# Input projection of a hybrid encoder block: the first and the last 512 tokens taken slice by slice of features

## The chip, the cores and the metric

The kernel runs on one core of one Trainium2 chip, in one launch. The metric is the device time of a whole execution in microseconds. Before the change it is 2899.7 us, the median of three runs (2899.47, 2899.7 and 2901.88).

## What is computed

One encoder block on x, 2048 tokens of 1024 features, all in float32. Only the first lines bear on the change:

```python
xn = rms_norm(h, ln_mix_g[l])
proj = xn @ w_in[l]                      # 2048 x 2512
y_a = mlstm_group(proj[..., OFF_Q:OFF_K], ..., proj[..., OFF_G:OFF_CQ] + b_gates[l], ...)
y_b = mla_group(proj[..., OFF_CQ:OFF_CKV], proj[..., OFF_CKV:OFF_KR], proj[..., OFF_KR:IN_COLS], ...)
```

The last 464 columns of `proj`, called "rest" here, are 16 gate columns, 256 columns of c_q, 128 of c_kv and 64 for the rotary key. `mla_group` applies an RMS norm to c_q and c_kv, and a rotary embedding to the 64. Then come attention, the mLSTM, the output projection, a gated MLP with convolution and a per-layer embedding; the change leaves these alone.

## The kernel before

Tokens stand in 16 tiles of 128 and features in 8 slices of 128. A float32 product is made of three matmuls in a faster 32-bit format: each operand is split into a high part (a cast on ScalarE) and a low part (the difference, on VectorE), and `mm3` (L131) issues low x high, high x low, high x high. The gain of the norm is multiplied into the weights while they are split (`split_g`, L125), and the factor of a token, r = (mean of x^2 + eps)^-1/2, is multiplied in when a product leaves PSUM. A column of these factors is called `rcol`.

`in_proj` (L176) multiplies the same x with three groups of weights one after the other: rest (464 columns), V and O (512 each). Products go to four PSUM banks, `bk`, used in turn. For the rest group the loop of L303 has a step for each token tile:

- `load_x` (L221) loads the turned tile of x, features on partitions (512 KB, `x_t`), one step ahead, and `split_x` (L242) splits it in two halves of 512 elements (L120 on ScalarE, L123 on VectorE).
- `ssq_x` (L228) makes rcol of the tile before: squares on ScalarE (L231), two additions on VectorE (L233, L234), four small matmuls with a column of ones on TensorE (`ssp`, L237), a scale on VectorE (L239), and a power of -1/2 on GpSimd (L240).
- `rest` (L248) issues the 24 matmuls of the tile two steps back (`nat`, L212) and takes the bank out: two gate writes `gt` on VectorE (L252), the scaled copy `rs` on ScalarE (L255), the load of the rotary table `sc` (L257), two squares with sums `ssq` on ScalarE (L261, L262), three small operations on GpSimd for their reciprocal roots (L263, L141, L143), two normed products `nn` on VectorE (L265, L266), a store of `vv_d`, and seven small rotary operations on VectorE (L269 to L275). The bank is free once `gt` and `rs` have read it.
- `turn_rest` (L278), four steps back, transposes the four blocks of `nn` on TensorE into `rtp` (L281), copies them out on ScalarE as `rt` (L283), and stores `rest_d` (256 KB).

After the loop rcol is stored to `r_d` (L320, 2048 single elements), and the V and O groups run 16 tiles of 24 matmuls each; two of the turns stand in the V group. The code's order is a priority: the framework's scheduler places each instruction on its engine's queue, and each queue is then executed in order. All loads and stores are issued on SyncE's queue (SP). `gates()` is a generator of side work on the gate columns that is advanced between the V and O tiles.

Of the kernel before, what the change touches and what calls it, by code (L numbers as in the profile page):

```python
# [19 lines left out]
P = 128  # L20
S = 2048
D = 1024
KT = D // P
NT = S // P
# [3 lines left out]
OFF_V = 1024  # L28
OFF_O = 1536
OFF_R = 2048  # L30
NREST = W_IN_COLS - OFF_R
# [2 lines left out]
PLE = 256  # L34
EPS = 1e-6
SB = 512
LAG_T, LAG_X, LAG_R = 1, 2, 2
SIDE = 668
KSCALE = 128.0 ** -0.5
ASCALE = 192.0 ** -0.5  # L40
# [20 lines left out]
class Block:  # L61
# [114 lines left out]
    def in_proj(self):  # L176
        nc, d = self.nc, self.d
# [5 lines left out]
        def load_w(c0, n, before=None):  # L183

            out, raws = [], []

            def load(k2, parts=1):
                raw = self.at(next(rrot), [P, 2, 512], name="wraw")
                for i in range(parts):
                    bs = slice(2 * i // parts, 2 * (i + 1) // parts)  # L190
                    nc.sync.dma_start(raw[:, bs, :n], w_in[k2, :, bs, c0:c0 + n])
                raws.append(raw)
                return raw

            if before:
                load(0, 2)
                before(0)
                load(1, 2)
                before(1)
                load(2)  # L200
                load(3)
            for k2 in range(KT // 2):
                if k2 == len(raws):
                    load(k2)
                raw = raws[k2]
                for b in range(2):
                    w = self.at(next(wrot), [P, 2, 512], F32R, "wsp")
                    self.split_g(raw[:, b, :n], gcol[:, 2 * k2 + b:2 * k2 + b + 1], w[:, 0, :n], w[:, 1, :n])
                    out.append(w)
            return out  # L210
# [10 lines left out]
        def load_x(st):  # L221

            t = self.at(next(rrot) if st else "u2", [P, KT, P], name="x_t")
            if st:
                nc.sync.dma_start(t, d["x_turned"][:, :, st * P:(st + 1) * P])
            return t

        def ssq_x(st, x_t):  # L228

            sq = self.at("w13", [P, KT, P], name="x_sq")  # L230
            nc.scalar.activation(sq, x_t, AF.Square)  # L231
            ss = self.at("t7", [P, 4, P], name="x_ss")
            nc.vector.tensor_tensor(ss, sq[:, 0:4], sq[:, 4:8], op=ALU.add)  # L233
            nc.vector.tensor_tensor(ss[:, 0:2], ss[:, 0:2], ss[:, 2:4], op=ALU.add)  # L234
            ps = self.pml.tile([P, 4], F32, name="ssp", tag="ml")
            for i in range(2):
                nc.tensor.matmul(ps, ss[:, i], ones, start=i == 0, stop=i == 1)  # L237
            t = self.stat(1, "rsm")
            nc.vector.tensor_scalar(t, ps[:, 0:1], 1.0 / D, EPS, op0=ALU.mult, op1=ALU.add)  # L239
            nc.gpsimd.tensor_tensor(rcol[:, st:st + 1], t, self.nhalf[:, :1], op=ALU.pow)  # L240

        def split_x(st, x_t):  # L242
            c, o = st // 4, (st % 4) * P
            for f in range(2):
                self.split(x_t[:, 4 * f:4 * f + 4], xh[c][f][:, :, o:o + P], xl[c][f][:, :, o:o + P])


        def rest(st):  # L248
            ps = nat(st, ws, NREST)
            rx = rcol[:, st:st + 1]  # L250
            for i, o in ((0, st), (8, NT - 1 - st)):
                nc.vector.scalar_tensor_tensor(self.gt[:, i:i + 8, o], ps[:, i:i + 8], rx, bg[:, i:i + 8],  # L252
                                               op0=ALU.mult, op1=ALU.add)
            rs = self.at(f"t{st % 2}", [P, 448], name="rs")
            nc.scalar.activation(rs, ps[:, 16:NREST], AF.Copy, scale=rx)  # L255
# [5 lines left out]
            nc.scalar.activation(nn[:, 0:256], rs[:, 0:256], AF.Square, scale=1.0 / 16.0, accum_out=ssq[:, 0:1])  # L261
            nc.scalar.activation(nn[:, 256:384], rs[:, 256:384], AF.Square, accum_out=ssq[:, 1:2])  # L262
            nc.gpsimd.tensor_scalar(ssq[:, 1:2], ssq[:, 1:2], 1.0 / 128, None, op0=ALU.mult)  # L263
            r = self.rsq(ssq, 2, 1.0)
            nc.vector.scalar_tensor_tensor(nn[:, 0:256], rs[:, 0:256], r[:, 0:1], gn[:, 0:256], op0=ALU.mult, op1=ALU.mult)  # L265
            nc.vector.scalar_tensor_tensor(nn[:, 256:384], rs[:, 256:384], r[:, 1:2], gn[:, 256:384], op0=ALU.mult, op1=ALU.mult)  # L266
            nc.sync.dma_start(self.vv_d[:, st], nn[:, 256:384])
# [7 lines left out]
            nc.vector.tensor_copy(nn[:, 448:512], nn[:, 384:448])  # L275
            return nn

        def turn_rest(st, nn):  # L278
# [8 lines left out]
        nc.sync.dma_start(gcol, d["g_turned"])  # L287
        rcol = self.cst.tile([P, NT], F32, name="rcol")
        ones = self.cst.tile([P, 4], F32, name="ones")
        nc.vector.memset(ones, 1.0)  # L290
        nq, xq = {}, {}

        xq[0] = load_x(0)

        def first(f):

            fs = slice(4 * f, 4 * f + 4)
            if f < 2:
                nc.sync.dma_start(xq[0][:, fs], d["x_turned"][:, fs, 0:P])
                self.split(xq[0][:, fs], xh[0][f][:, :, 0:P], xl[0][f][:, :, 0:P])  # L300

        ws = load_w(OFF_R, NREST, first)
        for st in range(NT + LAG_X):  # L303
            if st + 1 < NT:
                xq[st + 1] = load_x(st + 1)
            if st == 0:
                gn = self.at("t5", [P, 384], name="gn")
                self.row_bcast(gn[:, 0:256], d["q_norm_g"][0], 256)
                self.row_bcast(gn[:, 256:384], d["kv_norm_g"][0], 128)
                bg = self.row_bcast(self.cst.tile([P, 16], F32, name="bg"), d["b_gates"][0], 16)  # L310
            if 1 <= st < NT:
                split_x(st, xq[st])
            if 0 <= st - 1 < NT:
                ssq_x(st - 1, xq.pop(st - 1))
            if 0 <= st - LAG_X < NT:
                nq[st - LAG_X] = rest(st - LAG_X)
            if 0 <= st - LAG_X - LAG_R < NT:
                turn_rest(st - LAG_X - LAG_R, nq.pop(st - LAG_X - LAG_R))

        nc.sync.dma_start(self.r_d.rearrange("(t p) -> p t", p=P), rcol)  # L320
        gates = self.gates()

        ws = load_w(OFF_V, 512)
        for st in range(NT):
            ps = nat(st, ws, 512)
            if st < LAG_R:
                turn_rest(NT - LAG_R + st, nq.pop(NT - LAG_R + st))
# [3 lines left out]
            if st >= LAG_R:  # L331
                next(gates, None)

        ws = load_w(OFF_O, 512)
# [1709 lines left out]
```

## Time and profile before

| | us |
|---|---|
| median of three runs | 2899.7 |
| the profiled execution's own time | 2898.51 |
| its span in the trace | 2896.7 |
| first matmul of the rest group starts | 7.40 |
| first matmul of the V group starts | 106.63 |
| TensorE busy in the span | 2854.7 |
| VectorE, ScalarE, GpSimd busy | 2029.8, 1524.2, 157.1 |

The granted TensorE clock is 0.998 of full speed. A row of the trace's timeline gives start, duration, engine, line, operation and `out<-in`, and a bracket with the idle time before it and what ended that. The time in which TensorE is busy is summed over matmuls that overlap, so the pace of a stage is read from start to start.

### The profile page before, as it was taken

What the parts mean: (1) busy time and instruction counts of PE and PEld (TensorE: products, weight loads), DVE (VectorE), ACT (ScalarE), POOL (GpSimd) and SP (SyncE); (2) the same over time, 40 slices, a digit from 0 to 9 for tenths busy, and PEclk for the clock granted to TensorE, in tenths of its full rate; (3) what the DMA queues carried; (4) which work ended last, traced back from release to release, by engine and by line L of the source; (5) the groups of instructions that cost most, each with busy time, mean ns of one, the idle gap of its engine ahead of it and who ended that gap; (6) DMA issues with size and microseconds to landing.
All of it is one profiled execution on the core that took longest, in us unless ns stands there. A gap on an engine that the chain in (4) does not pass through costs nothing.

```text
span 2896.7 us, 41145 instructions
## 1 busy us (share of the span) xinstructions
PE 2854.7 (99%) x14622; PEld 2416.9 (83%) x14622; DVE 2029.8 (70%) x3758; ACT 1524.2 (53%) x3014; POOL 157.1 (5%) x295
## 2 busy tenths in 40 slices
PE   8999999999999999999999999999999999999998
PEld 7888888888888889888788888888888788888787
DVE  7521555777777777776777877867777867676787
ACT  7311544556666666665755555655556333254665
POOL 3100000000000010001000000000000000011111
PEclk9999999999999999999999999999999999999999
DMA  6512545653332333378844554657766757576764
GB/s 189 132 59 77 162 125 163 218 162 117 105 111 98 97 104 113 126 244 267 276 145 165 193 174 147 220 176 235 234 230 210 241 187 249 166 265 205 263 217 163
DMA packets 408318, 509.00 MB, mean 176 GB/s; under 512 B 34080, under 2 KB 271664, under 8 KB 408112
## 3 DMA queue, kind: packets, MB, share of 16 engines
q1 hardware_dynamic: 408112, 506.37, 53.8%
q8 instruction: 115, 1.88, 0.3%
q14 instruction: 91, 0.75, 0.1%
HBM read 324.16 MB, written 182.12 MB: 175 GB/s over the span
## 4 chain that ended last, share of the span: by engine, by line
PE 58%; DMA 3%; DVE 3%; issue 2%; ACT 2%; POOL 0%; POOLq 0%; SPq 0%; ACTq 0%; DVEq 0%
PE fy L1434 21%; PE fz L1434 14%; PE fx L1434 14%; PE ppv L133 2%; PE fs L133 1%; PE tb L977 1%; DMA opr<-t_d 1%; DMA h_d<-xt 1%; PE bk L914 1%; PE bk L916 1%; PE bk L915 1%; PE bk L917 1%; PE bk L918 1%; DMA opr<-tw_d 1%; DVE op L123 1%
## 5 line engine op out<-in xcount | busy, mean ns | idle before, releaser
L1434 PE MATMUL fz<-op,fw 128*128 128x512 f32 x1968 | 478.8, 391 | 4.5 <-ACT fw L120 4.0
L1434 PE MATMUL fx<-op,fw 128*128 128x512 f32 x1968 | 476.4, 390 | 0.0
L1434 PE MATMUL fy<-op,fw 128*128 128x512 f32 x1968 | 475.3, 390 | 0.6 <-ACT fy L1546 0.6
L1434 PEld LDWEIGHTS fz<-op,fw 128*128 128x128 f32 x1968 | 368.4, 188 | 82.4 <-ACT fw L120 5.4
L1434 PEld LDWEIGHTS fy<-op,fw 128*128 128x128 f32 x1968 | 368.6, 188 | 77.3 <-ACT fy L1546 1.0
L1434 PEld LDWEIGHTS fx<-op,fw 128*128 128x128 f32 x1968 | 368.2, 188 | 76.1 <-ACT fy L1546 0.2
L1434 PE MATMUL fy<-op,fwd 128*128 128x512 f32 (+1 forms) x984 | 238.2, 390 | 1.9 <-DVE uv L1419 1.5
L120 ACT CAST pt<-tb 128x512 fp32r<-128x512 f32 x256 | 147.3, 587 | 172.1 <-PE tb L977 171.5
L133 PE MATMUL bk<-wsp,xh 128*128 128x512 f32 (+1 forms) x768 | 234.3, 386 | 0.0
L919 DVE TENSOR_REDUCE mx<-bk 128x1 f32<-128x512 f32 x256 | 174.8, 684 | 59.8 <-PE bk L918 58.8
L1434 PEld LDWEIGHTS fy<-op,fwd 128*128 128x128 f32 x984 | 182.6, 188 | 40.6 <-DVE uv L1419 2.6
L133 PE MATMUL ppv<-pt,kv 128*128 128x256 f32 x1536 | 205.2, 287 | 0.4 <-DVE pt L123 0.3
L123 DVE TENSOR_TENSOR pt<-tb,pt 128x512 fp32r<-128x512 f32 x256 | 173.9, 683 | 31.4 <-ACT pt L120 29.2
L937 ACT ACTIVATE pe<-bk,nm 128x512 f32<-128x512 f32 x256 | 174.8, 695 | 37.8 <-DVE nm L931 33.0
L133 PEld LDWEIGHTS ppv<-pt,kv 128*128 128x128 f32 x1536 | 189.3, 191 | 0.9 <-DVE pt L123 0.5
L133 PEld LDWEIGHTS bk<-wsp,xh 128*128 128x128 f32 x768 | 145.3, 189 | 25.0
L133 PE MATMUL bk<-wsp,xl 128*128 128x512 f32 (+1 forms) x384 | 150.6, 392 | 7.4 <-DVE xl L123 7.4
L133 PE MATMUL bk<-xh,wqk 128*128 128x512 f32 x480 | 157.1, 393 | 0.0
L977 PE MATMUL tb<-ident,pe 128*128 128x128 f32 x1024 | 151.0, 273 | 3.8 <-DVE pt L123 3.7
L977 PEld LDWEIGHTS tb<-ident,pe 128*128 128x128 f32 x1024 | 121.7, 140 | 23.4 <-DVE pt L123 6.0
L120 ACT CAST fw<-hraw 128x1024 fp32r<-128x1024 f32 (+1 forms) x72 | 70.2, 980 | 115.7 <-PE fx L1434 58.7
L120 ACT CAST op<-opr 128x512 fp32r<-128x512 f32 x165 | 95.9, 621 | 58.3 <-DMA opr<-tw_d 17.6
(360 smaller groups left out, 4915.3 us busy)
## 6 DMA issues: line engine op xcount, KB each, us to landing
fwr<-in_w_up SPq DMA_DIRECT2D x66, 512.0 KB, 5.2
fh<-h_d SPq DMA_DIRECT2D x48, 512.0 KB, 4.3
h_d<-fh SPq DMA_DIRECT2D x48, 512.0 KB, 4.1
s_d<-fwr SPq DMA_DIRECT2D x44, 512.0 KB, 3.2
fws<-s_d SPq DMA_DIRECT2D x44, 512.0 KB, 3.5
rw<-row_d SPq DMA_DIRECT2D x32, 512.0 KB, 5.1
tw_d<-tsum SPq DMA_DIRECT2D x60, 256.0 KB, 5.3
opr<-tw_d SPq DMA_DIRECT2D x60, 256.0 KB, 5.1
```

What stands on the lines that cost most here:

```text
L120: nc.scalar.copy(hi, src)
L123: (sub or nc.vector).tensor_tensor(lo, src, _f(hi), op=ALU.subtract)
L133: mm = lambda *a, **k: self.nc.tensor.matmul(*a, **k, skip_group_check=more)
L914: mm(ps, ql, kh[:, ks], start=True, stop=False)
L915: mm(ps, qr, self.krl[:, ks], start=False, stop=False)
L916: mm(ps, qh, kl[:, ks], start=False, stop=False)
L917: mm(ps, qr, self.kr2[:, ks], start=False, stop=False)
L918: mm(ps, qh, kh[:, ks], start=False, stop=True)
L919: nc.vector.tensor_reduce(s.mx[:, kb:kb + 1], ps, axis=AX.X, op=ALU.max)
L937: nc.scalar.activation(s.pe[:, kb % 2], s.banks[kb], AF.Exp, bias=s.nm, scale=ASCALE, accum_out=s.rs[:, kb:kb + 1])
L977: nc.tensor.transpose(t[:, j, :], s.p[kb][:, j * P:(j + 1) * P], self.ident)
L1434: nc.tensor.matmul(out, a[:, k * P:(k + 1) * P], parts[lo][:, cols], start=first, stop=lo == 1 and k == last, skip_group_check=more)
```

## The change

The rest group is ordered by hand: inside `manual_schedule` TensorE, VectorE and ScalarE keep the order of the code, while SP and GpSimd are still placed by the scheduler. The parts:

- The first four token tiles and the last four are each computed as one block (`block4`): all four banks at once, slice by slice of features, 96 matmuls. For the first block x arrives as 8 slices of 512 tokens (`x_c`, 256 KB each) between the weights' loads, and each slice is split as it is needed. In the last block the V weights are split step by step.
- The other tiles of x arrive by pairs: 256 tokens in two halves of the features (`x_p`, 512 KB each), each split with one cast and one difference of 1024 elements, at written places: the pair of tiles 4 and 5 ahead of the first eviction, the others behind the evictions of tiles 2, 4, 6, 7 and 8.
- rcol is made from a second copy of x, rows of tokens (`x_n`, 512 KB a tile, two buffers): one square on ScalarE of 1024 elements with a sum along the row, then a scale and a power on GpSimd. The additions on VectorE and the `ssp` matmuls are gone.
- The eviction of tile s stands behind the products of tile s+2, with the squares of its rows directly ahead of it. In it the rotary operations stand ahead of the two `nn`.
- The turn of tile s stands ahead of the products of tile s+5; turns 9, 10 and 11 stand inside the last block; the evictions and turns of tiles 12 to 15 stand in the V group, as does the store of `r_d`.
- Eight matmuls of the identity and a one-element activation stand at the start; `gcol` (the gain) is loaded by ScalarE's queue instead of SP's. The side work `gates` is first advanced four V tiles later.

```diff
-        def ssq_x(st, x_t):
-            sq = self.at("w13", [P, KT, P], name="x_sq")
-            nc.scalar.activation(sq, x_t, AF.Square)
-            ss = self.at("t7", [P, 4, P], name="x_ss")
-            nc.vector.tensor_tensor(ss, sq[:, 0:4], sq[:, 4:8], op=ALU.add)
-            nc.vector.tensor_tensor(ss[:, 0:2], ss[:, 0:2], ss[:, 2:4], op=ALU.add)
-            ps = self.pml.tile([P, 4], F32, name="ssp", tag="ml")
-            for i in range(2):
-                nc.tensor.matmul(ps, ss[:, i], ones, start=i == 0, stop=i == 1)
-            t = self.stat(1, "rsm")
-            nc.vector.tensor_scalar(t, ps[:, 0:1], 1.0 / D, EPS, op0=ALU.mult, op1=ALU.add)
-            nc.gpsimd.tensor_tensor(rcol[:, st:st + 1], t, self.nhalf[:, :1], op=ALU.pow)
+        def load_pair(p):
+            for f in range(2):
+                raw = self.at(next(rrot), [P, 4, 256], name="x_p")
+                nc.sync.dma_start(raw, d["x_turned"][:, 4 * f:4 * f + 4, p * 256:(p + 1) * 256])
+                xq[p, f] = raw
+        def load_rows(st):
+            t = xn[st] = self.at(("w13", "u2")[st % 2], [P, D], name="x_n")
+            nc.sync.dma_start(t, d["x"][0, st * P:(st + 1) * P, :])
+        def ssq_x(st):
+            ss = self.stat(1, "x_ss")
+            nc.scalar.activation(self.at("t7", [P, D], BF16, "x_sq"), xn.pop(st), AF.Square, accum_out=ss)
+            self.rsq(ss, 1, 1.0 / D, rcol[:, st:st + 1])
+        def block4(c, step):
+            ps = [self.bank() for _ in range(4)]
+            for kt in range(KT):
+                f, k = divmod(kt, 4)
+                step(kt)
+                w, x = ws[kt], ((xh, 0), (xl, 0), (xh, 1))
+                order = [(n, st) for st in range(4) for n in range(3)]
+                for n, st in order if c or kt else sorted(order):
+                    o, e = x[n]
+                    nc.tensor.matmul(ps[st][:, :NREST], o[c][f][:, k, st * P:(st + 1) * P], w[:, e, :NREST],
+                                     start=kt == 0 and n == 0, stop=kt == KT - 1 and n == 2)
+            done.update(enumerate(ps, 4 * c))
...
+        with self.tc.manual_schedule(engines={ET.PE, ET.DVE, ET.Activation}):
+            for _ in range(8):
+                nc.tensor.matmul(wp, self.ident, self.ident, start=True, stop=True)
+            raws, xr = first_loads()
+            block4(0, first_step)
...
+            ssq_x(0)
+            load_rows(2)
+            load_pair(3)
+            for f in range(2):
+                split_pair(2, f)
+            ssq_x(1)
+            load_rows(3)
+            evict(0)
+            evict(1)
+            loads, splits = {4: 4, 6: 5, 8: 6, 9: 7}, {4: 3, 6: 4, 8: 5, 9: 6, 10: 7}
+            for st in range(4, NT - 4):
+                if st in loads:
+                    load_pair(loads[st])
+                if st > 4:
+                    turn(st - 5)
+                done[st] = nat(st, ws, NREST)
+                ssq_x(st - 2)
+                load_rows(st)
+                evict(st - 2)
+                if st in splits:
+                    for f in range(2):
+                        split_pair(splits[st], f)
+            raws, wv = load_w(OFF_V, 512), []
+            for st in range(NT - 4, NT - 2):
+                turn(st - 5)
+                ssq_x(st - 2)
+                load_rows(st)
+                evict(st - 2)
+            for st in range(NT - 2, NT):
+                ssq_x(st - 2)
+                load_rows(st)
+            block4(3, last_step)
...
+            if st < 4:
+                evict(NT - 4 + st)
+            ps = nat(st, wv, 512)
+            if 2 <= st < 6:
+                turn(NT - 6 + st)
+            if st == 3:
+                nc.sync.dma_start(self.r_d.rearrange("(t p) -> p t", p=P), rcol)
```

More of the change, by code (lines that the diff above doesn't have):

```diff
@@ L181, in in_proj, with load_w, split_w @@
         w_in = d["w_in"][0].rearrange("(a b p) c -> a p b c", b=2, p=P)
[L183 to L201, printed above, removed]
-            for k2 in range(KT // 2):
[L203 to L210, printed above, removed]
+        def load_w(c0, n):
+            raws = []
+            for k2 in range(KT // 2):
+                raws.append(self.at(next(rrot), [P, 2, 512], name="wraw"))
+                nc.sync.dma_start(raws[k2][:, :, :n], w_in[k2, :, :, c0:c0 + n])
+            return raws
+        def split_w(raws, kt, n):
+            w = self.at(next(wrot), [P, 2, 512], F32R, "wsp")
+            self.split_g(raws[kt // 2][:, kt % 2, :n], gcol[:, kt:kt + 1], w[:, 0, :n], w[:, 1, :n])
+            return w
         def nat(st, ws, n):
@@ L242, in split_x @@
-        def split_x(st, x_t):
-            c, o = st // 4, (st % 4) * P
-            for f in range(2):
-                self.split(x_t[:, 4 * f:4 * f + 4], xh[c][f][:, :, o:o + P], xl[c][f][:, :, o:o + P])
-        def rest(st):
-            ps = nat(st, ws, NREST)
+        def load_pair(p):
+            for f in range(2):
+                raw = self.at(next(rrot), [P, 4, 256], name="x_p")
+                nc.sync.dma_start(raw, d["x_turned"][:, 4 * f:4 * f + 4, p * 256:(p + 1) * 256])
+                xq[p, f] = raw
@@ new lines, in split_pair @@
+        def split_pair(p, f):
+            c, o = p // 2, p % 2 * 256
+            self.split(xq.pop((p, f)), xh[c][f][:, :, o:o + 256], xl[c][f][:, :, o:o + 256])
+        def load_rows(st):
[5 more added lines that the diff above has]
+            self.rsq(ss, 1, 1.0 / D, rcol[:, st:st + 1])
@@ new lines, in first_loads @@
+        def first_loads():
+            raws, xr = [], []
+            for kt in range(KT):
+                if kt % 2 == 0:
+                    raws.append(self.at(next(rrot), [P, 2, 512], name="wraw"))
+                xr.append(self.at(f"t{kt}", [P, 512], name="x_c"))
+                if kt < 2:
+                    nc.sync.dma_start(raws[0][:, kt, :NREST], w_in[0, :, kt, OFF_R:OFF_R + NREST])
+                    if kt == 0:
+                        nc.scalar.dma_start(gcol, d["g_turned"])
+                elif kt % 2 == 0:
+                    nc.sync.dma_start(raws[kt // 2][:, :, :NREST], w_in[kt // 2, :, :, OFF_R:OFF_R + NREST])
+                nc.sync.dma_start(xr[kt], d["x_turned"][:, kt, 0:512])
+            load_rows(0)
+            load_pair(2)
+            load_rows(1)
+            return raws, xr
@@ new lines, in block4 @@
+        def block4(c, step):
+            ps = [self.bank() for _ in range(4)]
+            for kt in range(KT):
+                f, k = divmod(kt, 4)
[7 more added lines that the diff above has]
+            done.update(enumerate(ps, 4 * c))
@@ L250, in rest @@
+        def rest(st, ps):
             rx = rcol[:, st:st + 1]
@@ L275, in rest @@
             nc.vector.tensor_copy(nn[:, 448:512], nn[:, 384:448])
+            nc.vector.scalar_tensor_tensor(nn[:, 0:256], rs[:, 0:256], r[:, 0:1], gn[:, 0:256], op0=ALU.mult, op1=ALU.mult)
+            nc.vector.scalar_tensor_tensor(nn[:, 256:384], rs[:, 256:384], r[:, 1:2], gn[:, 256:384], op0=ALU.mult, op1=ALU.mult)
+            nc.sync.dma_start(self.vv_d[:, st], nn[:, 256:384])
             return nn
@@ L286, in in_proj @@
         gcol = self.cst.tile([P, KT], F32, name="gcol")
-        nc.sync.dma_start(gcol, d["g_turned"])
         rcol = self.cst.tile([P, NT], F32, name="rcol")
[L289 to L318, printed above, removed]
@@ L320, in in_proj, with evict, turn, first_step @@
-        nc.sync.dma_start(self.r_d.rearrange("(t p) -> p t", p=P), rcol)
+        warm = self.stat(1, "warm")
+        nc.scalar.activation(warm, self.nhalf[:, 0:1], AF.Copy, scale=2.0)
+        wp = self.pml.tile([P, P], F32, name="warm", tag="ml")
+        nq, xq, xn, done, ws = {}, {}, {}, {}, []
+        ET = mybir.EngineType
+        def evict(st):
+            nq[st] = rest(st, done.pop(st))
+        def turn(st):
+            turn_rest(st, nq.pop(st))
+        def first_step(kt):
+            f, k = divmod(kt, 4)
+            ws.append(split_w(raws, kt, NREST))
+            self.split(xr[kt], xh[0][f][:, k, :], xl[0][f][:, k, :])
@@ new lines, in last_step @@
+        def last_step(kt):
+            if kt in (0, 2):
+                ssq_x(NT - 2 + kt // 2)
+            wv.append(split_w(raws, kt, 512))
+            if kt in (2, 4, 6):
+                turn(NT - 8 + kt // 2)
+        with self.tc.manual_schedule(engines={ET.PE, ET.DVE, ET.Activation}):
[3 more added lines that the diff above has]
+            block4(0, first_step)
+            gn = self.at("t5", [P, 384], name="gn")
+            self.row_bcast(gn[:, 0:256], d["q_norm_g"][0], 256)
+            self.row_bcast(gn[:, 256:384], d["kv_norm_g"][0], 128)
+            bg = self.row_bcast(self.cst.tile([P, 16], F32, name="bg"), d["b_gates"][0], 16)
+            ssq_x(0)
[30 more added lines that the diff above has]
+            block4(3, last_step)
@@ L330, in in_proj @@
             nc.sync.dma_start(self.v_d[st], t)
-            if st >= LAG_R:
+            if st >= 6:
                 next(gates, None)
-        ws = load_w(OFF_O, 512)
+        raws = load_w(OFF_O, 512)
+        ws = [split_w(raws, kt, 512) for kt in range(KT)]
         go = self.row_bcast(self.at("t6", [P, 512], name="go"), d["mlstm_norm_g"][0], 512)
```

13 lines of the change are left out of this document (removed).

## The prediction

> **What bounds the kernel now.** I read the page first, then the busy times of the stretch that the change touches, then TensorE's waits in it.
>
> ```profile
> span 2896.7 us, 41145 instructions
> ...
> PE 2854.7 (99%) x14622; PEld 2416.9 (83%) x14622; DVE 2029.8 (70%) x3758; ACT 1524.2 (53%) x3014; POOL 157.1 (5%) x295
> ```
> ```profile
> 7.40:106.60 99.20, 96.92 (x503) 86.03 (x504) 70.36 (x256) 67.71 (x149) 35.71 (x61) 1.00 0.68 167
> ```
> ```profile
> PE bk L133 <- DVE xl L123: 7.4, 1, 7.4
> PE ssp L237 <- DVE x_ss L234: 2.2, 3, 1.1
> ```
>
> The second row is the rest group: 99.20 us, then busy time (and count) of PE, PEld, DVE, ACT, POOL, then clock, DMA share and GB/s. TensorE (PE) is the bound, 99% in the whole and 96.92 of 99.20 here; it waits 7.4 us for its first operand and 2.2 us later. VectorE (DVE) and ScalarE (ACT) are busy 70%. Everything behind the group is unchanged and PE-bound, so I carry the shift of the V group's start to the end 1:1. How PE spends a steady tile:
>
> ```profile
> 53.60 0.60 PE L281 MATMUL rtp<-ident,nn 128*128 128x128 f32 x4
> 54.04 0.51 PE L237 MATMUL ssp<-ones,x_ss 128*128 128x4 f32 x4
> 54.40 0.45 PE L133 MATMUL bk<-wsp,xl 128*128 128x464 f32 x1
> 59.50 0.60 PE L281 MATMUL rtp<-ident,nn 128*128 128x128 f32 x4
> 106.63 0.48 PE L133 MATMUL bk<-wsp,xl 128*128 128x512 f32 x1
> ```
>
> From start to start a turn takes 0.44, the sums of squares 0.36, the 24 products 5.10 (0.21 each): 5.90 us a tile. The group has 16 x 5.10 + 14 x 0.44 + 16 x 0.36 = 93.5 of its 99.2 us; 5.7 are a slow start and short waits. The V group starts at 106.63.
>
> **What the change takes off PE.** The `ssp` matmuls go: 5.8 us. Two more turns move into V: 0.9 off here, 0.9 on there. The start:
>
> ```profile
> 4.03 1.28 ACT L128 ACT_TABLE_LOAD   x1 [4.03 <-DMA wraw<-in_w_in]
> 5.33 0.68 ACT L128 ACTIVATE wsp<-wraw,gcol 128x464 fp32r<-128x464 f32 x1
> 8.72 0.59 PE L133 MATMUL bk<-wsp,xl 128*128 128x464 f32 x1
> 9.88 0.59 PE L133 MATMUL bk<-wsp,xl 128*128 128x464 f32 x1
> 12.15 0.37 PE L133 MATMUL bk<-wsp,xl 128*128 128x464 f32 x1
> ```
>
> The one-element activation pulls the table load under the first transfer, which lands at 4.03. Then one weight split (0.68) and one cast (0.62, from the row below) give the first product at 4.0 + 0.7 + 0.6 = 5.3 instead of 7.40, as the new order begins with high x high. Three products take 1.16 us until about 12 (8.72 to 9.88), against 0.63 later: over the 4.6 us of the slow start some 2.0 us are lost. The eight identity matmuls are to save these. By the four of 53.60 they last about 1 us warm, 2 cold, and would end two to three us ahead of the first product, while the trace's own products needed 4.6 us of unbroken work. I charge 1.0, half of it, with ends 0 and 2.0.
>
> The Trainium skill ("TensorE: Matmul & The Clock Gate", "Part 1: The HAM clock gate") says full rate follows about 3.4 us of sustained activity in a free-running window; by that rule the identity matmuls do nothing, and the sum would be 1.0 higher.
>
> If PE alone set the time, V would start at 5.3 + 1.0 + 16 x 5.10 + 12 x 0.44 = 93.2, 13.4 us early. The question is whether tiles are evicted fast enough.
>
> **What the written order makes of the eviction.** ScalarE now runs, in this order for each tile: `rt` of an older tile, squares of x rows, `rs`, two squares; behind five of the tiles two casts of 1024. The squares of rows feed GpSimd (POOL), whose power feeds `gt` and `rs` of the same tile. So one tile's eviction begins only after the earlier one's squares, and this ring has these durations:
>
> ```profile
> 24.15 0.35 DVE L252 SCALAR_TENSOR_TENSOR gt<-bk,rcol,bg 128x8 f32<-128x8 f32 x2
> ...
> 24.62 0.63 ACT L255 ACTIVATE rs<-bk,rcol 128x448 f32<-128x448 f32 x1 [1.31 <-DVE gt L252]
> ```
> ```profile
> 54.61 1.28 DVE L123 TENSOR_TENSOR xl<-x_t,xh 128x512 fp32r<-128x512 f32 x2
> ...
> 56.31 0.92 POOL L240 TENSOR_TENSOR rcol<-rsm,nhalf 128x1 f32<-128x1 f32 x1 [2.40 <-DVE rsm L239]
> ...
> 58.07 0.58 ACT L283 COPY rt<-rtp 128x512 f32<-128x512 f32 x1
> ...
> 58.54 0.43 ACT L261 ACTIVATE nn<-rs 128x256 f32<-128x256 f32 x1
> ...
> 59.15 0.20 ACT L262 ACTIVATION_READ_ACCUMULATOR nn<-rs 128x1 f32 x1
> 59.24 1.05 ACT L231 ACTIVATE x_sq<-x_t 128x1024 f32<-128x1024 f32 x1
> ...
> 59.44 0.22 POOL L263 TENSOR_SCALAR ssq<-ssq 128x1 f32<-128x1 f32 x1 [2.21 <-ACT nn L262]
> ...
> 60.02 0.73 POOL L143 TENSOR_TENSOR rsr<-rsm,nhalf 128x2 f32<-128x2 f32 x1
> ...
> 60.19 0.61 ACT L120 CAST xh<-x_t 128x512 fp32r<-128x512 f32 x1
> ```
>
> `gt` to `rs` 0.47; `rs` 0.63; both squares 0.70 (58.54 to 59.24); `rt` 0.47 (58.07 to 58.54); row squares 1.05 and 0.1 for the sum; POOL's scale 0.3 (59.44 to 60.02 holds two such operations); power 0.92; then the next `gt`. Sum 4.64, say **4.6 us**. PE's own step is 5.10 + 0.44 = 5.54, so a tile without a split keeps up. With a split two casts stand ahead of `rt`: a 1024-element pass takes 0.95 from start to start (59.24 to 60.19), so 1.9 more: **6.5 us**. VectorE's two differences, 2.5 us by four halves of 54.61, lie beside that. The old code's split was as much work, but nothing made the tile's `rcol` wait for it. DVE loses the two additions and L239, which were no bound.
>
> From the first `rs` to that of tile 11 are 11 steps, 6 plain and 5 with a split: 27.6 + 32.5 = 60.1 us. The last block needs all four banks, and its fourth is tile 11's, so this ring, not PE, sets when the block can run.
>
> Two terms come on top. First, POOL beside VectorE:
>
> ```profile
> L263 POOL TENSOR_SCALAR ssq<-ssq x16: 222/224/1296, 21.4 to 111.8; 128x1 f32<-128x1 f32 x16
> ```
> ```profile
> 44.47 1.30 POOL L263 TENSOR_SCALAR ssq<-ssq 128x1 f32<-128x1 f32 x1 [0.53 <-ACT nn L262]
> ...
> 45.00 0.68 DVE L123 TENSOR_TENSOR xl<-x_t,xh 128x512 fp32r<-128x512 f32 x1
> ```
>
> The same tiny operation takes 0.22 us at the median and 1.30 at worst (first row: minimum, median, maximum in ns), and the worst ends with the difference that runs beside it (45.68). In the new order POOL's scale for `rcol` falls under the 1024-element differences in all five split steps. Ends 0 and 1.1 each; I take 0.5, as the operation falls anywhere in a difference: **2.5 us**.
>
> The Trainium skill ("SBUF — State Buffer", "Who interferes with whom") has it that a VectorE operation with two SBUF inputs and a GpSimd operation that reads SBUF exclude each other, the later one blocking fully. The 1.30 agrees, and it speaks against this change; taken at its full length in all five steps, the sum would be 3 us higher.
>
> Second, transfers:
>
> ```profile
> DMA packets 33310, 18.56 MB, mean 169 GB/s; under 512 B 5598, under 2 KB 31829, under 8 KB 33299
> ...
> x_t<-in_x_turned SPq DMA_DIRECT2D x15, 512.0 KB, 4.2
> ...
> rest_d<-rt SPq DMA_DIRECT2D x13, 256.0 KB, 8.9
> ...
> sc<-in_rope SPq DMA_DIRECT2D x16, 32.0 KB, 2.0
> ```
> ```profile
> 10.00:20.00 10.00, 9.57 (x44) 7.89 (x43) 8.74 (x20) 8.36 (x13) 1.65 (x2) 1.00 1.02 285
> ```
>
> The first view covers 0 to 110 us. x is loaded twice now: 16 x 512 KB add 8.4 MB to 18.56. Full engines moved 285 GB/s at 10 to 20, so 27 MB fill some 95 of 110 us: little slack. In SP's new queue the rotary table of tile 10 stands behind the store of tile 9's `vv_d`, four V weight loads and a row load. The store can go when `nn` of tile 9 is done, some 3.5 us after its `rs`; six issues at about 0.5 and a 2.0 landing bring the table at 8.5, where tile 10's rotary operations could use it at 4.6 + 0.6 = 5.2, and these stand ahead of `nn` and the next `gt` on VectorE: 3 us late. The first table costs some 0.5 likewise. I take **3.5 us**, ends 0 and 9 (one landing of 8.9).
>
> **The sum.** Bank 0 is done when 87 of the first block's 96 products are: 5.3 + 1.0 + 87 x 0.21 = 24.6; `rs` of tile 0 at 25.1; of tile 11 at 25.1 + 60.1 + 2.5 + 3.5 = 91.2; its bank free at 91.8. Then 87 products (18.3), three turns (1.3), and a wait in the last block: the turn of tile 10 needs the buffer that ScalarE's copy of tile 9's turn clears, and that copy stands behind the row squares of tiles 14 and 15, whose loads are issued only after tile 11's rotary operations. Counted from tile 11's `rs` the copy ends at 1.5 (rotary) + 0.5 + 4.2 (issue and landing as for `x_t`) + 2.5 (the second load) + 1.05 + 0.7 (square, weight split) + 0.6 = 11.0; PE is there at 0.6 + 39 products + one turn = 9.3: 1.7. V starts at 113.0, 6.4 later than 106.63; two more turns in V make 7.3. Against the profiled execution's 2898.51 that is 2905.8, and this lies 1.2 under the median of the runs, so I forecast **2907.0 us**.
>
> Put at nothing: the V weights' split, 8 x 0.68 = 5.4 us of ScalarE beside the last block's 20 (uncovered, V's start is late by up to that); the evictions of tiles 12 to 15 in V, 1.8 us of ScalarE each beside 24 products (a ring step of 4.6 if a bank waits for one); `gcol` on ScalarE's queue and the side work that starts four tiles later, which nothing on PE waits for in V.
>
> **Rivals.** *The ring hides* (faster): the first block ends at 24.6 + 1.9 = 26.5, the eight tiles between the blocks take PE 8 x 5.54 = 44.3, and from 25.1 to 70.8 the ring has 45.7 us for 11 steps. So it decides from 4.2 us a step: if ScalarE, GpSimd and VectorE overlap more than I read, PE sets the time, V starts at 93.2, 12.5 early with the V turns, and the time is 2887. For it speaks that the plain step is near, 4.6; against it the five splits, which make the mean 5.5. *Ring without extras* (no change): no POOL delay, quick tables, warm start: 7 less, 2900. *Transfers bind*:
>
> ```profile
> 100.00:110.00 10.00, 10.00 (x52) 8.72 (x51) 6.57 (x24) 6.74 (x14) 1.15 (x3) 1.00 1.19 70
> ```
>
> with `r_d` in the queues the engines are full at 70 GB/s; if rows and pairs land late by one such landing (8.9) at tile 10 or 14, or the V evictions wait for tables behind `r_d`: 2916. *The warm-up does nothing*: 1.0 more, 2908.
>
> **How the numbers follow.** Forecast with the warm-up case 0.45; ring without extras 0.25; transfers 0.18; ring hides 0.12. A measurement tells 0.2% (5.8 us) from no change: slower means over 2905.5. Faster 0.12; the same holds the second case and some of the first, 0.30; slower 0.58. The range leaves out the ring that hides and little above: 2894 to 2918.
>
> **What would show it.** `rs` of tile 11 near 91, waits of PE of some 20 us in all between 27 and 92, most of them at the last block's banks, split steps of 6.5 to 7 us against 4.6, first product near 5.3. Wrong if PE's waits between 25 and 90 sum to under 8 us, or if `rs` waits for something else than `rcol` or `gt`.

## The result, and the profile after

The changed kernel takes 2910.27 us (median of 15 runs, 2905.56 to 2917.76) against 2900.24 before (15 runs, 2897.05 to 2904.26): ratio 1.0035, 95% interval 1.0028 to 1.0041. It is slower by 10.0 us, where 7.3 were forecast. The first rows of the page of the changed kernel, and the waits of TensorE (PE) up to 130 us (engine, line, what it waited for: us in total, times, longest):

```profile
span 2907.4 us, 41027 instructions
...
PE 2856.2 (98%) x14574; PEld 2415.0 (83%) x14574; DVE 2016.8 (69%) x3697; ACT 1528.7 (53%) x3019; POOL 156.1 (5%) x311
```
```profile
PE bk L255 <- ACT rs L265: 8.0, 1, 8.0
PE rtp L291 <- ACT rt L293: 7.6, 4, 4.6
PE warm L324 <- POOL ident masks.py:199: 1.3, 1, 1.3
PE bk L132 <- DVE xl L122: 0.9, 3, 0.3
```

TensorE is busy nearly as long as before (2856.2 against 2854.7), and its idle time in the span grows by 9.2 us (51.2 against 42.0), so the loss is nearly all waiting, not work. The wait for the first operand is gone from this list, and behind the start 16.5 us of waiting have come: 15.6 for ScalarE (ACT), for its copy of a turn (L293) and for its copy out of a bank (L265), and 0.9 for VectorE. Line 265 is `rs`, 293 is `rt`, 223 the squares of the rows, 119 a cast, 122 a difference, 140 and 142 GpSimd's scale and power. TensorE's start and the milestones of the stage:

```profile
1.16 1.28 ACT L299 ACT_TABLE_LOAD   x1 [1.16 <-PEq L2069]
1.34 3.78 PE L324 MATMUL warm<-ident 128*128 128x128 f32 x16 [1.34 <-POOL ident masks.py:199]
...
4.83 1.91 PE L255 MATMUL bk<-wsp,xh 128*128 128x464 f32 x4
6.55 1.33 PE L255 MATMUL bk<-wsp,xl 128*128 128x464 f32 x4
...
93.51 0.75 PE L255 MATMUL bk<-wsp,xh 128*128 128x464 f32 x1 [7.99 <-ACT rs L265]
...
98.70 0.59 PE L255 MATMUL bk<-wsp,xl 128*128 128x464 f32 x1
...
115.80 0.39 PE L132 MATMUL bk<-wsp,xl 128*128 128x512 f32 x1
```

The first product starts at 4.83 instead of 7.40, and V at 115.80 instead of 106.63: 9.2 late. Two more turns in V make 10.1, and the first Q/K matmul, behind V and O, starts at 293.3 against 283.3. So in these two executions what the stage lost reached the end nearly unchanged.

Next, two steps of the eviction, the first with a split, the second without (one answer of the timeline, 45.5 to 58 us):

```profile
45.74 0.64 ACT L265 ACTIVATE rs<-bk,rcol 128x448 f32<-128x448 f32 x1 [1.57 <-DVE gt L262]
...
47.12 1.99 ACT L119 CAST xh<-x_p 128x1024 fp32r<-128x1024 f32 x2
...
49.30 2.36 DVE L122 TENSOR_TENSOR xl<-x_p,xh 128x1024 fp32r<-128x1024 f32 x2
...
49.48 1.06 ACT L223 ACTIVATE x_sq<-x_n 128x1024 bf16<-128x1024 f32 x1
...
50.72 0.99 POOL L140 TENSOR_SCALAR rsm<-x_ss 128x1 f32<-128x1 f32 x1 [2.12 <-ACT x_sq L223]
...
52.84 0.64 ACT L265 ACTIVATE rs<-bk,rcol 128x448 f32<-128x448 f32 x1 [2.21 <-DVE gt L262]
...
54.69 1.06 ACT L223 ACTIVATE x_sq<-x_n 128x1024 bf16<-128x1024 f32 x1
...
55.92 0.35 POOL L140 TENSOR_SCALAR rsm<-x_ss 128x1 f32<-128x1 f32 x1 [0.22 <-ACT x_sq L223]
...
57.40 0.64 ACT L265 ACTIVATE rs<-bk,rcol 128x448 f32<-128x448 f32 x1 [1.57 <-DVE gt L262]
```

From `rs` to `rs` it is 7.10 with a split and 4.56 without; the other steps up to tile 10 repeat these two numbers to 0.04, but for the first (4.17). With a split the squares begin 3.74 after `rs`, without one 1.85: the two casts, 1.89. The rest is GpSimd's scale, 0.99 against 0.35: it ends (51.71) when VectorE's differences do (51.66).

The last step, from tile 10 to tile 11, takes 9.52. The queue of loads (SP) and VectorE (DVE) there:

```profile
82.42 0.33 SPq L285 DMA_DIRECT2D vv_d<-nn  x1
82.79 0.83 SPq L187 DMA_DIRECT2D wraw<-in_w_in  x1
...
83.72 0.52 SPq L294 DMA_DIRECT2D rest_d<-rt  x1
84.33 0.58 SPq L218 DMA_DIRECT2D x_n<-in_x  x1
84.95 0.47 SPq L267 DMA_DIRECT2D sc<-in_rope  x1
...
90.84 0.19 DVE L276 TENSOR_TENSOR sc<-rs,sc 128x32 f32<-128x32 f32 x1 [7.63 <-DMA sc<-in_rope]
...
92.37 0.36 DVE L262 SCALAR_TENSOR_TENSOR gt<-bk,rcol,bg 128x8 f32<-128x8 f32 x2
```

The 32 KB of tile 10's rotary table are issued behind the store of `vv_d`, a weight load, a store and a load of rows, and VectorE can go on with them 5.9 us later. It has then waited 7.63 for them, and tile 11's `gt` stands behind it.

### The profile page after: what moved, and what is told of

It reads as the page before. It is cut to its first block, busy times and chain, and to the rows that moved or that the text cites. A ratio compares the mean times of both kernels' runs of the same rounds, so it can differ in the third digit from the quotient of the medians.

```text
span 2907.4 us, 41027 instructions
## 1 busy us (share of the span) xinstructions
PE 2856.2 (98%) x14574; PEld 2415.0 (83%) x14574; DVE 2016.8 (69%) x3697; ACT 1528.7 (53%) x3019; POOL 156.1 (5%) x311
## 4 chain that ended last, share of the span: by engine, by line
PE 58%; DMA 3%; DVE 3%; ACT 2%; issue 2%; POOL 0%; SPq 0%; POOLq 0%; ACTq 0%; DVEq 0%
PE fy L1480 21%; PE fz L1480 14%; PE fx L1480 13%; PE ppv L132 2%; PE fs L132 2%; PE tb L1023 1%; DMA opr<-tw_d 1%; DMA opr<-t_d 1%; PE bk L960 1%; PE bk L962 1%; PE bk L961 1%; PE bk L963 1%; PE bk L964 1%; DMA h_d<-xt 1%; DVE op L122 0%
## 5 line engine op out<-in xcount | busy, mean ns | idle before, releaser
L132 PE MATMUL bk<-wsp,xh 128*128 128x512 f32 (+1 forms) x640 | 195.1, 386 | 0.0
L132 PEld LDWEIGHTS bk<-wsp,xh 128*128 128x128 f32 x640 | 120.2, 188 | 22.4
L132 PE MATMUL bk<-wsp,xl 128*128 128x512 f32 (+1 forms) x320 | 125.3, 391 | 0.9 <-DVE xl L122 0.9
```

Source lines behind the costliest of these rows:

```text
L132: mm = lambda *a, **k: self.nc.tensor.matmul(*a, **k, skip_group_check=more)
```

## The experiments

My theory: ScalarE's written order, with GpSimd and VectorE, is a ring that hands tile after tile on in 4.6 or 7.1 us, and TensorE waits for its last tile. The rivals: transfers set the pace, as x is loaded twice; or the blocks are slow by themselves. All times of the stage below are from one profiled execution each, medians and ratios to before from the timed runs. The kernels were timed in groups on different chips, each group with before beside it (medians 2898.93 to 2901.39): a ratio is taken within its group, and medians of different groups can be compared only to some 2 us.

| kernel | rs of tile 0 | rs of tile 11 | V starts | median us | ratio to before, 95% interval |
|---|---|---|---|---|---|
| before | | | 106.63 | 2900.24 | |
| changed | 25.30 | 92.82 | 115.80 | 2910.27 | 1.0035, 1.0028 to 1.0041 |
| e1_tables | 24.23 | 86.57 | 111.15 | 2908.69 | 1.0025, 1.0013 to 1.0037 |
| e2_squares | 24.15 | 87.08 | 110.08 | 2905.1 | 1.0019, 1.0010 to 1.0029 |
| e3_rows_once | 24.48 | 86.84 | 108.69 | 2905.25 | 1.0018, 1.0009 to 1.0028 |
| e4_clock | 24.52 | 93.16 | 115.14 | 2908.04 | 1.0025, 1.0016 to 1.0034 |
| e5_ring_open | 24.22 | 74.05 | 95.86 | 2895.56 | 0.9979, 0.9971 to 0.9988 |
| e6_no_warm | 26.30 | 92.05 | 115.98 | 2916.11 | 1.0054, 1.0039 to 1.0070 |
| e7_before_start | | | 106.16 | 2898.86 | 0.9992, 0.9983 to 1.0001 |
| e8_both | 24.15 | 82.44 | 108.46 | 2905.95 | 1.0018, 1.0009 to 1.0027 |
| e9_subs_later | 24.60 | 91.58 | 114.32 | 2910.51 | 1.0034, 1.0022 to 1.0046 |
| e10_tiles_last | 24.33 | 91.95 | 107.77 | 2911.81 | 1.0040, 1.0025 to 1.0054 |
| e11_open_rows_once | 25.57 | 75.61 | 98.54 | 2892.55 | 0.9973, 0.9963 to 0.9982 |
| e12_open_no_warm | 26.44 | 76.48 | 98.38 | 2898.52 | 0.9991, 0.9982 to 1.0000 |

**Tables earlier (e1).**

```diff
 def evict(st):
     nq[st] = rest(st, done.pop(st))
+    if st + 2 < NT:
+        load_tab(st + 2)        # the load of sc, taken out of rest()
```

> The rotary table of each tile is loaded two evictions ahead instead of in its own eviction. Ring theory (ScalarE's written order, GpSimd and VectorE form a ring of 4.6 us for a plain tile and 7.1 for one with a split, and TensorE waits for its last tile): the steps stay 4.6 and 7.1, the step from tile 10 to tile 11 falls from 9.5 to 4.6, rs of tile 11 starts near 87.9 instead of 92.8, V starts near 111 instead of 115.8, about 2905 us. Transfer theory (x loaded twice fills the DMA engines and sets the pace): the wait moves to another load, rs of tile 11 stays at 91 to 93, 2909 to 2911 us.

Steps stay 4.6 and 7.1, the last falls from 9.52 to 4.56, V starts at 111.15: as the ring has it. The late table cost 5.0 us at its step, and V starts 4.65 earlier. The median falls by 1.6 only, to 2908.69 where 2905 was expected; why so little arrives is not shown.

**Squares ahead of the casts (e2).**

```diff
-    ssq_x(st - 2)
-    load_rows(st)
     evict(st - 2)
+    ssq_x(st - 1)
+    load_rows(st + 1)
     if st in splits:
```

> The squares of a tile's rows stand one tile earlier on ScalarE, behind the eviction of the tile before and ahead of the casts of a split. Ring theory: the casts are no longer between a tile's eviction and the next tile's factor, so a plain step falls from 4.6 to about 4.1 and a split step from 7.1 to about 6.4, where VectorE's two differences behind nn end it; GpSimd's scale for rcol no longer falls under the differences (0.99 us to 0.2 to 0.4). rs of tile 10 comes near 77.6 instead of 83.3, the late table of tile 10 stays, V starts near 110, about 2904.5 us. Transfer theory: row loads and pairs become the wait, 2909 to 2911 us.

Split steps fall to 6.28, near the 6.4 expected, and there `gt` follows VectorE's differences at once; V starts at 110.08. A plain step stays 4.56, where 4.1 was expected: GpSimd's three operations for `nn` stand ahead of its scale for rcol, so the earlier squares only wait there. The plain step thus has a second path of the same length, through GpSimd.

**Rows of x loaded once (e3).** Later rows are not loaded, so rcol of tiles 2 to 15 is that of tiles 0 and 1.

```diff
 def load_rows(st):
+    if st > 1:
+        xn[st] = kept[st % 2]
+        return
...
```

> Rows of x are loaded for tiles 0 and 1 only and their squares are taken again for all others (so rcol of the others is that of tiles 0 and 1): 7.3 of 28.3 MB less to move in the stage, every instruction of the engines kept. Ring theory: steps stay 4.6 and 7.1; only the table of tile 10 and the row squares of tiles 14 and 15 come sooner, V starts 2 to 4 us earlier, 2906 to 2908 us. Transfer theory: the stage shortens with the bytes, V starts 10 us earlier or more, 2900 us or less.

Its `rs` rows around two steps, and the waits that are left:

```profile
44.78 0.64 ACT L270 ACTIVATE rs<-bk,rcol 128x448 f32<-128x448 f32 x1 [1.57 <-DVE gt L267]
51.88 0.63 ACT L270 ACTIVATE rs<-bk,rcol 128x448 f32<-128x448 f32 x1 [2.22 <-DVE gt L267]
56.44 0.64 ACT L270 ACTIVATE rs<-bk,rcol 128x448 f32<-128x448 f32 x1 [1.56 <-DVE gt L267]
```

7.10 and 4.56 again, to the hundredth, with a quarter of the bytes gone: transfers do not set these steps. V starts 7.1 us earlier, between the 2 to 4 of the ring theory and the 10 of the transfer theory. Of this the late table, which is a transfer, is 5.0 (the step to tile 11 is 4.56) and an earlier tile 0 is 0.8; the remaining 1.3 I put down to earlier rows of tiles 14 and 15, which no run separates.

**The clock (e4).** Twenty identity matmuls on TensorE ahead of the fourth bank's first product.

```diff
+    if c and kt == 0 and st == 3 and n == 0:
+        for _ in range(20):
+            nc.tensor.matmul(wp, self.ident, self.ident, start=True, stop=True)
```

> Twenty identity matmuls more stand on TensorE in the wait ahead of the last block's fourth bank, some 7 us of work inside a wait of 8. Clock theory (TensorE idles from 76 to 81 and from 85.5 to 93.5 and so runs its next 15 products at 0.39 instead of 0.21): the products behind the wait run at 0.21 from the start, 2.8 us are won, of which 1.7 come back as a wait of the turn of tile 10 for ScalarE's copy; V starts about 1.1 earlier, 2909 us. Rival (something else slows these products, such as operands or banks): they stay at 0.39 and V starts at 115.8, 2910 us.

```profile
85.36 4.62 PE L256 MATMUL warm<-ident 128*128 128x128 f32 x40
93.85 0.48 PE L258 MATMUL bk<-wsp,xh 128*128 128x464 f32 x1 [3.86 <-ACT rs L268]
94.16 0.37 PE L258 MATMUL bk<-wsp,xl 128*128 128x464 f32 x1
...
95.76 0.59 PE L258 MATMUL bk<-wsp,xl 128*128 128x464 f32 x1
96.15 0.97 PE L258 MATMUL bk<-wsp,xh 128*128 128x464 f32 x2
```

The twenty took 4.62, not 7, so 3.86 of idle time stayed. The first products then run at 0.21, and from 95.0 on at 0.39 after all. With less idle time ahead of them the same products on the same operands and banks start at full pace, so idle time slows them, and with a delay. Up to tile 9's turn the 15 products take 4.8 instead of 5.9, and V starts 0.7 earlier.

**The ring taken apart (e5).** The tables of e1 and the squares of e2; one half of a pair cast behind each eviction, its difference in the next, and `nn` a tile later:

```diff
 def evict(st):
-    nq[st] = rest(st, done.pop(st))
+    half[st] = rest(st, done.pop(st))      # gt, rs, squares, rotary; sub_half() behind gt
+    if st + 2 < NT:
+        load_tab(st + 2)
+    if st - 1 in half:
+        nq[st - 1] = norm(st - 1, *half.pop(st - 1))    # the two nn and the store
...
     evict(st - 2)
+    ssq_x(st - 1)
+    load_rows(st + 1)
+    cast_half(st // 2 + 2, st % 2)
...
-            if kt in (0, 2):
-                ssq_x(NT - 2 + kt // 2)
+            if kt == 0:
+                ssq_x(NT - 2)
             wv.append(split_w(raws, kt, 512))
-            if kt in (2, 4, 6):
+            if kt == 6:
+                ssq_x(NT - 1)
+            if kt in (4, 6):
                 turn(NT - 8 + kt // 2)
```

> The ring is taken apart: tables two evictions ahead, row squares one tile ahead, the pairs split by halves, one cast behind each eviction from tile 0 to tile 9 and its difference in the next eviction between gt and the rotary operations, nn of a tile behind the rotary operations of the next, tile 9's turn ahead of the last block and the squares of tile 15 late in it. The blocks, the pairs and both loads of x stay. Ring theory: ScalarE's 4.0 to 4.3 us a tile is under TensorE's 5.5, TensorE sets the pace, its waits between 27 and 92 fall from 16 to under 5 us, V starts at 94 to 98 instead of 115.8, about 2890 us, faster than before. Transfer theory, or blocks that are slow by themselves: V cannot start before 105, 2900 us or more.

```profile
PE rtp L313 <- ACT rt L315: 2.9, 2, 2.2
```
```profile
44.64 0.64 ACT L285 ACTIVATE rs<-bk,rcol 128x448 f32<-128x448 f32 x1 [0.64 <-DVE gt L281]
...
49.19 0.64 ACT L285 ACTIVATE rs<-bk,rcol 128x448 f32<-128x448 f32 x1 [0.62 <-DVE gt L281]
...
69.77 0.64 ACT L285 ACTIVATE rs<-bk,rcol 128x448 f32<-128x448 f32 x1
74.05 0.64 ACT L285 ACTIVATE rs<-bk,rcol 128x448 f32<-128x448 f32 x1 [1.30 <-DVE gt L281]
```

Steps of 4.55 with half a split in each (5.45 and 5.48 ahead of the last one shown, near TensorE's own 5.54), waits down from 16.5 to 2.9, V at 95.86, 10.8 ahead of before, with both blocks and both loads of x kept. So neither the second load of x nor the blocks by themselves make the loss, though a late transfer, the table, was 5.0 us of it. It is the fastest version that does the whole work, 0.9979 of before, but 2895.56 where 2890 was expected. Of 10.0 us at the first Q/K matmul (273.3 against 283.3) only 5.8 are left in the medians (2901.39 for before in its group). Its profiled execution, the slowest of its eleven (2898.69), has lost nearly all: 4.0 us of TensorE's waits stand in the stage around 500 to 560 us, for VectorE's `kk`, against 1.0 in that of before, and the granted clock there is 0.91 in two stretches of 20 us. Why these waits grow was not tried and stays open.

**Tables and squares together (e8).** Both edits above.

> Only the tables two evictions ahead and the row squares one tile ahead, together. Ring theory: steps of 4.6 and 6.3 and no 7.6 or 9.5 at tile 11, rs of tile 11 near 84, V starts at 107 to 108.5, about 2902 us. Transfer theory: one of the gains is lost to another late load, V at 110 or later, 2905 us.

rs of tile 11 comes at 82.44, V at 108.46, the late end of what the ring gives: TensorE waits 8.8 us for copies of turns, among them 2.35 in the last block. The time (2905.95, where 2902 was expected) is no better than that of e2 alone, within the intervals.

**No identity matmuls (e6, and e12 from e5).** The loop of eight is taken out.

> Without the eight identity matmuls at the start (the activation that loads the table stays). If they warm the clock: the first block's products run at 0.39 for 4.6 us more, its end moves from 26.5 to about 28, rs of tile 0 from 25.3 to about 27, V starts up to 1.5 later, about 2911.5 us. If they do nothing: the first block ends at 26.5 and all stays, 2910 us.

> The opened ring (e5) without the eight identity matmuls. If they warm the clock, the first block ends some 2 us later, and with TensorE setting the pace this reaches the V group: V starts near 97.9 instead of 95.9, about 2897.5 us. If they do nothing, V starts at 95.9, 2895.5 us.

TensorE's start in e12:

```profile
8.15 2.13 PE L268 MATMUL bk<-wsp,xh 128*128 128x464 f32 x5
10.08 0.53 PE L268 MATMUL bk<-wsp,xl 128*128 128x464 f32 x1
10.45 0.59 PE L268 MATMUL bk<-wsp,xh 128*128 128x464 f32 x2
10.87 0.37 PE L268 MATMUL bk<-wsp,xl 128*128 128x464 f32 x1
```

Products run at 0.39 until 10; in the changed kernel, with the eight, they do so until about 7, and in e8 only the first takes longer. rs of tile 0 comes at 26.30 and 26.44 without the eight and at 24.15 to 25.57 in the kernels with them, so they are worth 1 to 2 us at tile 0. What of this reaches the end is less clear: e12 starts V 2.5 later than e5 and its median is 3.0 higher, but the intervals of the two ratios overlap, and e11, which has the eight, starts V as late as e12. In e6 V starts where it did (115.98): this time the table of tile 7 was late (VectorE waits 6.32 for it, and the step to tile 8 takes 10.48) and that of tile 10 not. Its median, of four runs, is 5.8 above the changed kernel's, which the stage does not explain; that stays open.

**The start alone, in the kernel before (e7).** Only the one-element activation and the gain's load on ScalarE's queue.

> The kernel before with one part of the change alone: the one-element activation at the start and the gain's load on ScalarE's queue. The table load (1.28 us) leaves the path of the first product: first product at 6.0 instead of 7.40, V starts some 1.4 us earlier than 106.63, about 2899 us; rival: the transfers of the first x tiles, not the first product, set the first 20 us, and V starts where it did.

First product at 6.68 where 6.0 was expected, V only 0.5 earlier, and the ratio's interval holds 1. TensorE is busy 0.6 us longer in the first 20 us (12.78 against 12.17) and 0.4 us shorter from 20 to 50 (27.77 against 28.15): an early first product alone is given back by the next tiles.

**Differences moved behind the next `gt` (e9).**

```diff
     gt(...)                     # two writes
+    sub_halves()                # both differences of the last split
     rs = ...
...
```

The load of the last pair moves behind its eviction as well.

> Only VectorE's two differences of a split move: from behind the eviction to the next eviction, between gt and the rotary operations; the two casts stay ahead of rt and the squares of rows. If the split step's 7.10 is 4.57 + 1.9 for the casts + 0.6 for GpSimd's scale standing still beside the differences (0.99 against 0.35 us), the scale falls to about 0.2, the split step to about 6.4, and the plain step behind a split grows by up to 0.5, since GpSimd's three operations for nn now stand beside the differences; rs of tile 11 1 to 3 us earlier, V at 113 to 115. If the differences cost nothing through GpSimd, split steps stay at 7.1 and V at 115.8.

```profile
51.30 0.19 POOL L140 TENSOR_SCALAR rsm<-x_ss 128x1 f32<-128x1 f32 x1 [2.80 <-ACT x_sq L236]
```

The scale for rcol falls to 0.19 and four of five split steps to 6.28 to 6.30; the steps behind them rise from 4.57 to 5.09 (one to 5.44). Both as expected: the 0.99 was GpSimd standing still beside the differences, and moving them brings it to other GpSimd operations. V at 114.32.

**The last four tiles as tiles (e10).**

```diff
-    block4(3, last_step)
+    for st in range(NT - 4, NT):
+        turn(st - 5)
+        done[st] = nat(st, ws, NREST)
+        ssq_x(st - 2)
+        load_rows(st)
+        evict(st - 2)
```

> The last four tiles of the rest group as single tiles of 24 products again, with their turns and evictions in the same rhythm as the others, the V weights split behind tile 14's eviction, one more turn in V; the first block, pairs, rows and the late table stay. If the wait ahead of the last block costs because a block needs four free banks at once: TensorE takes tiles 12 to 14 while tile 11's eviction is late, V starts at 102 to 106 instead of 115.8, about 2900 us. If only the ring counts (16 steps, then 5.4 us of weights on ScalarE), V starts at 112 or later, 2907 us or more.

```profile
104.10 1.11 PE L291 MATMUL rtp<-ident,nn 128*128 128x128 f32 x4 [4.05 <-ACT rt L293]
107.77 1.65 PE L132 MATMUL bk<-wsp,xl 128*128 128x512 f32 x3 [2.55 <-ACT wsp L127]
```

TensorE is through with the rest group at 99.5 instead of 115.6, since tiles 12 to 14 no longer need tile 11's bank. But then it waits for the copy of a turn and for the V weights, whose split stands behind tile 14's eviction on ScalarE. V starts at 107.77, between my two forecasts, at a low clock and with a further wait at 130 to 140, and the first Q/K matmul is at 293.3, exactly where the changed kernel has it. I read this so: the demand for four banks fixes where the wait is, the ring how long it is. It is not shown as sharply as that, since the V weights' split and a turn moved too, and the equal place of the first Q/K matmul may be chance.

**Rows once in the opened ring (e11).** e5 with the edit of e3, and the same part left out.

> The opened ring (e5) with rows of x loaded for tiles 0 and 1 only, their squares taken again for the others (so rcol of the others is that of tiles 0 and 1): 7.3 MB less to move. If TensorE sets the pace in e5, the second load of x is hidden: V starts within 1.5 us of 95.9, the total within 2 us of e5. If transfers hold back the steps of 5.5 or the waits of the last turns in e5: V starts 3 us earlier or more.

V starts at 98.54, not earlier but 2.7 later than in e5; 1.4 of that is there at tile 0, the rest arises behind tile 11. That misses both forecasts: a start of V within 1.5 us, and one 3 us earlier. The late tile 0 begins with a wait of 0.78 us of TensorE in the first block, for a cast of x. The median is 3.0 lower, with overlapping intervals, so in the stage the second load of x is hidden, and a gain outside it is not shown.

## Why the prediction was right

Direction and size were right: 2907.0 forecast, 2910.27 measured. The mechanism, a ring of evictions that TensorE waits for, was the one forecast; two of its terms were off, and the carry to the end was in part luck. By its steps:

- *The start.* Forecast first product 5.3, measured 4.83. One of two us of slow start charged; the first block took 21.65 (4.83 to 26.48) where 96 products at the later pace take 20.4: 1.2. That is right for this execution; in the other kernels with the eight (e11 aside, where TensorE waits in it) the block took 20.16 to 20.95, and without them 22.7. The identity matmuls were priced too short: sixteen records filled 3.78 us, not 1 to 2. The price came from the transposes of a turn, which are one record each, while a plain float32 matmul is two, as the `ssp` row shows (two matmuls in the code, four records). The Trainium skill's rule of about 3.4 us of sustained activity ("TensorE: Matmul & The Clock Gate", "Part 1: The HAM clock gate"), by which the prediction had them do nothing, speaks for them at this length of 3.78 us. e6 and e12 agree with it: 1 to 2 us at tile 0.
- *rs of tile 0.* 25.1 forecast, 25.30 measured. The same start gave 24.15 to 25.57 in the other kernels, so agreement to 0.2 is luck.
- *The ring.* Plain step 4.6: measured 4.56 to 4.60. Split step 6.5 and 0.5: measured 7.10, with 1.89 for the casts where 1.9 was forecast. e2 and e9 move only the order and the split step moves with it; e3 takes away a quarter of the bytes and it stays. That the plain step came out to 0.1 is partly luck, as its parts offset each other: from GpSimd's power to `gt` it is 0.58 where 0.92 was charged, from its scale to the power 0.44 where 0.3 was, from the row squares to the scale 1.23 where 1.15 was. What the sum did not have is the second path of the plain step, through GpSimd's operations for `nn`, which e2 showed to be as long.
- *GpSimd beside VectorE.* 0.5 a split, 2.5 in all: measured 0.64 each (0.99 against 0.35), 3.2. The rule of the Trainium skill ("SBUF — State Buffer", "Who interferes with whom"), that a VectorE operation with two SBUF inputs and a GpSimd operation that reads SBUF exclude each other, agrees with this. In e9 the scale takes 0.19 with no difference beside it.
- *Transfers.* 3.5 for the tables: 4.9 measured, all at tile 10 (9.52 against 4.58). The place was right, the size a third too small: VectorE could use the table 5.9 us after its issue, not 2.0. This term was mis-sized.
- *rs of tile 11.* 91.2 forecast, 92.82 measured.
- *The last block.* Forecast from the bank's release: 87 products, three turns and a wait of 1.7. That wait did not come (in e1 one of 1.28 for such a copy does); instead the clock fell, which no step had. The 15 products from 93.51 to tile 9's turn took 5.9 instead of 3.1, 2.8 more, and in that time ScalarE's copy caught up. So a term of 2.8 stands where one of 1.7 was, and V starts at 115.80 where 113.0 was forecast.
- *Waits.* Some 20 us in all forecast, 16.5 measured. Most of them were to stand at the last block's banks; 8.0 do, and 7.6 stand at copies of turns, which the forecast did not name there.
- *The carry to the end.* 1:1 forecast. From the first Q/K matmul to the end of the span it is 2613.4 us before and 2614.1 in the changed kernel, but 2612.0 (e4) to 2623.6 (e5) in the others, where nothing behind V and O was changed. So the carry holds to several us only, and that it held to 0.7 here is luck.

## What to carry to other kernels

When a schedule is written by hand, write down for each engine the chain from one tile's result to the next tile's first operation; it counts at its full length, with whatever stands between on that engine, and has to stay under the step of the engine that sets the pace. Work that nobody waits for (here casts) belongs behind the operation that the next tile waits for, in pieces that fit the gap, and small loads ahead of large ones in the queue. A wait that is removed at one place can come back at the next as long as the chain is the same, as in e10.

## What the runs showed of the hardware

The granted clock can fall after quite short waits of TensorE, and with a delay. In the changed kernel:

```profile
80.00:90.00 10.00, 4.81 (x13) 3.40 (x13) 1.60 (x7) 4.68 (x13) 3.97 (x10) 0.67 0.86 280
90.00:100.00 10.00, 6.49 (x20) 5.57 (x21) 3.52 (x20) 4.79 (x12) 2.92 (x7) 0.53 0.50 151
```

The clock column is 0.67 and 0.53 in these stretches, where TensorE idles 8 us. In e8 a single wait of 2.35 us was enough: the products behind it ran at 0.21 for half a us and then at 0.39. But not every wait of this length does it. The same matmuls behind the same kind of wait, first in e9, then in e5:

```profile
569.27 0.71 PE L829 MATMUL mb<-v,kk 128*128 128x129 f32 x4 [2.24 <-DVE kk L822]
...
570.28 3.12 PE L132 MATMUL ppv<-pt,kv 128*128 128x256 f32 x24
```
```profile
554.37 0.76 PE L854 MATMUL mb<-v,kk 128*128 128x129 f32 x4 [2.49 <-DVE kk L847]
...
555.74 4.25 PE L132 MATMUL ppv<-pt,kv 128*128 128x256 f32 x24
```

Behind 2.24 us the clock stays at 1.00 (569 to 573) and the 24 products take 3.12; behind 2.49 us it is 0.50 from 556 to 558 and they take 4.25. So a wait of some 2 us can cost more than its length. What decides whether it does is not shown.
